# The opening of a hybrid decoder layer: norm sums from rows of tokens, one chunk unnormed, three products side by side

## The chip, the cores and the metric

The kernel runs on one core of a Trainium2 chip. The metric is the device time of one execution in microseconds (us), the median over runs. A core has five engines that take instructions in their own order and wait for each other through semaphores: TensorE (PE in the profile; its weight loads are PEld), VectorE (DVE), ScalarE (ACT), GpSimd (POOL) and SyncE (SP, which only issues DMAs here). GpSimd and ScalarE issue some DMAs too.

## The reference

One layer over 1,024 prompt tokens and 64 sample tokens (T = 1088), model width 1024, all in float32. The part that matters here is its beginning:

```
xn = rmsnorm(x, norm1_g)                  # x * rsqrt(mean(x*x) + eps) * g, per token
proj = xn @ w_in                          # q | k | v | glu_a | glu_b | gate_a | gate_b
u = glu_a * sigmoid(glu_b)                # then causal depthwise conv (31), layernorm, silu, w_pb
h = x + (sigmoid(gate_a) * A + sigmoid(gate_b) * B) @ w_out    # A: windowed attention, B: the conv branch
y = h + ConvFFN(rmsnorm(h))               # up, conv (3), silu gate, down; final rmsnorm
```

## The kernel before

Activations lie transposed: 128 channels on the partitions, tokens along the free axis, in KT = 8 slices k of the 1024 channels. Tokens are cut into three chunks of 384, 384 and 320 columns (`CHUNKS`). Every float32 operand is split into a high part (rounded to the matmul's type by a copy on ScalarE, `xh`, `whi`) and the rest (a subtraction on VectorE, `xl`, `wlo`); a product of one 128-column weight unit with one chunk is 24 matmuls, three per k: `wh*xh`, `wh*xl`, `wl*xh` (L183 to L185, `mm3`). A product over all three chunks is 72 matmuls. `SEQUENCE` gives the order of the input projection's 44 units: `b` and `a` are the two halves of the GLU, `g` gates, `q0` and `q1` queries, `k`, `v`. A `b`/`a` pair is followed by a depthwise convolution on VectorE (L452 and neighbours), which runs beside later products.

The opening is the first `FIRST` = 5 units, worked chunk by chunk rather than unit by unit, since x is not normed yet. `norm1_load` brings x by DMA on SyncE's queue, chunk 0 in pieces between the pieces of the first two weights; `norm1_raw` scales x by g only and splits it (L253, L254). The products run on that, and the factor 1/rms of the token (`rstd`) is multiplied in when a result leaves PSUM (`ev_b`, `ev_a`, `ev_q`, `gate_evac` with `self.scale`). `norm1_stats` makes the factor: squares on ScalarE (L263), their sum over k on VectorE (L265), the sum over partitions by a matmul with a constant matrix (L268), square root and a reciprocal over 128 x 384 elements (L283, L284). In chunk 0 the first two products run side by side, k by k, while x is still landing (`stream_side`). After each chunk's products the earlier chunk is normed in place for the 39 units that follow (`norm1`: L277 on VectorE, L278 on ScalarE, L280 in turn on VectorE and GpSimd). The last one, chunk 2, is normed after the fifth product.

The order on each engine is the tile framework's: it places instructions by priority, in the order of the program text, shifted by `later`; `issue_after` (new in the change) holds an instruction back behind a named one. An engine runs its own list strictly in order. PSUM has eight banks, four under the tag `mm` and four under `aux` (`FIRST_TAGS` deals them out); a product waits until its bank has been emptied. In the opening the raw weights lie in borrowed tiles (`u`, `c`), and the fifth split weight in the unused end of the query tiles `q`.

Of the kernel before, what the change touches and what calls it, by code (L numbers as in the profile page):

```python
# [12 lines left out]
P = 128  # L13
# [100 lines left out]
class Build:  # L114
# [29 lines left out]
    def w_split(self):  # L144
        if len(self.w_hl) < len(self.order):
            for go in self.w_parts(2 if len(self.w_hl) < FIRST else 1):
                go()
# [75 lines left out]
    def norm1_load(self, pp, c):  # L223
# [8 lines left out]
        self.w_raw += [self.t(self.wp, [P, DM], "wraw", bufs=2) for _ in range(2)]  # L232
        half = DM // 2
        w_part = lambda i, x: load(self.w_raw[i][:, x * half:(x + 1) * half], self.a["wall"][i][:, x * half:(x + 1) * half])
# [11 lines left out]
    def norm1_raw(self, c, xr, xh, xl):  # L246
        parts = list(zip(self.w_parts(W_PARTS), self.w_parts(W_PARTS))) if c == 0 else []
        for k in range(KT):
            if parts and k * W_PARTS % KT == 0:
# [7 lines left out]
    def norm1_stats(self, pp, c, xr):  # L257
        nc = self.nc
        n = CHUNKS[c][1]
        ps = self.bank("aux")  # L260
        for k in range(KT):
            sq = self.t(pp, [P, 384], "sq", bufs=SQ_BUFS)
            nc.scalar.activation(sq[:, :n], xr[:, k, :], AF.Square)  # L263
            if k:
                nc.vector.tensor_tensor(sq[:, :n], sq[:, :n], last[:, :n], ALU.add)  # L265
            last = sq
        with self.later(MEAN_LATER[c]):
            nc.tensor.matmul(ps[:, :n], self.mean, last[:, :n], start=True, stop=True)  # L268
        rstd = self.t(pp, [P, 384], f"rstd{c}")
        self.rstd(rstd[:, :n], ps[:, :n])  # L270
        return rstd

    def norm1(self, c, xr, rstd, xh, xl):
        nc = self.nc
        for k in range(KT):
            x = xr[:, k, :]
            nc.vector.scalar_tensor_tensor(x, x, self.c("g1", k), rstd[:, :CHUNKS[c][1]], ALU.mult, ALU.mult)  # L277
# [1175 lines left out]
```

## Time and profile before

| | |
|---|---|
| median of 3 runs | 1692.3 us (1691.95 to 1692.46) |
| the profiled execution | 1690.92 us, of which the span of instructions 1689.1 us |
| mean granted TensorE clock over the span | 0.997 |
| TensorE, VectorE, ScalarE, GpSimd busy | 1669.8, 1299.2, 842.3, 249.2 us |

The page gives busy time per engine, the chain of waits, the costliest groups of instructions by line, and the DMA issues. Other views of the same trace are a timeline of an engine, groups by line in a stretch, and a table of windows: for each stretch the busy time of each engine (with the count of instructions), the granted clock, the busy share of the 16 DMA engines, and GB/s. Matmuls overlap, so TensorE's "busy" is not a rate: what it does in a stretch is read from the number of matmuls.

### The profile page before, as it was taken

The page shows a single profiled execution, that of the slowest core. Times are in us where ns is not written, and L with a number is a line of the kernel's source. Part 1 is how long each engine was busy: PE and PEld are TensorE (multiplying, and loading weights), DVE is VectorE, ACT ScalarE, POOL GpSimd, SP SyncE. Part 2 cuts the span into 40 slices and gives each one's busy share as a digit, 9 for nine tenths or more (in the row PEclk, how much of TensorE's full clock was granted, in tenths as well). Part 3 has the DMA queues.
Part 4 walks back from the last instruction along what each step waited for, and adds up shares of the span by engine and source line. Part 5 has one row for each costly group of instructions (what it writes and reads, how often), then busy time and mean ns, then how long its engine had stood idle before and what let it go on. Part 6 is the DMA issues. An engine that isn't in the chain of part 4 may idle for free.

```text
span 1689.1 us, 29120 instructions
## 1 busy us (share of the span) xinstructions
PE 1669.8 (99%) x11372; PEld 1650.8 (98%) x11372; DVE 1299.2 (77%) x2265; ACT 842.3 (50%) x1711; POOL 249.2 (15%) x430
## 2 busy tenths in 40 slices
PE   9899999999999999999999999999999999999998
PEld 8899999999999999999999999999999999999997
DVE  8999989999679996865546887777777787754437
ACT  7424478753588745973233544444444455211102
POOL 1300212240011111110000261222222220000000
PEclk9999999999999999999999999999999999999999
DMA  6022212232211255644343333222222225843103
GB/s 209 30 63 71 74 62 98 82 123 58 82 45 51 78 215 170 178 152 151 110 144 106 93 106 103 78 77 78 78 77 78 90 66 164 257 119 103 52 1 106
DMA packets 103657, 172.16 MB, mean 102 GB/s; under 512 B 44336, under 2 KB 69312, under 8 KB 103504
## 3 DMA queue, kind: packets, MB, share of 16 engines
q1 hardware_dynamic: 89952, 125.15, 25.1%
q0 software_dynamic: 13424, 45.15, 7.3%
q8 instruction: 89, 1.46, 0.4%
q14 instruction: 48, 0.39, 0.1%
q10 hardware_dynamic: 144, 0.00, 0.0%
HBM read 124.74 MB, written 47.50 MB: 102 GB/s over the span
## 4 chain that ended last, share of the span: by engine, by line
PE 82%; DVE 11%; ACT 5%; issue 1%; DMA 1%; SPq 0%; DVEq 0%; ACTq 0%
PE mm L185 20%; PE mm L183 20%; PE mm L184 20%; PE aux L183 6%; PE aux L185 6%; PE aux L184 5%; DVE c L452 2%; ACT p L305 1%; DVE bt L452 1%; PE aux L338 1%; PE aux L351 1%; PE aux L350 1%; ACT p L309 1%; DVE xr L277 1%; PE aux L328 1%
## 5 line engine op out<-in xcount | busy, mean ns | idle before, releaser
L183 PE MATMUL mm<-xh,whi 128*128 128x384 f32 (+1 forms) x920 | 306.8, 334 | 5.0 <-DVE gt L649 2.3
L184 PE MATMUL mm<-xl,whi 128*128 128x384 f32 (+1 forms) x920 | 301.9, 328 | 0.7 <-DVE xl L254 0.5
L185 PE MATMUL mm<-xh,wlo 128*128 128x384 f32 (+1 forms) x920 | 300.9, 327 | 1.4 <-DVE wlo L165 1.4
L183 PEld LDWEIGHTS mm<-xh,whi 128*128 128x128 f32 x920 | 173.4, 189 | 7.4 <-ACT xh L278 2.6
L184 PEld LDWEIGHTS mm<-xl,whi 128*128 128x128 f32 x920 | 173.6, 189 | 3.0 <-DVE xl L254 1.9
L185 PEld LDWEIGHTS mm<-xh,wlo 128*128 128x128 f32 x920 | 173.1, 188 | 1.8 <-DVE wlo L165 1.7
L183 PE MATMUL mm<-mh,whi 128*128 128x272 f32 (+2 forms) x464 | 137.8, 297 | 0.0
L184 PE MATMUL mm<-ml,whi 128*128 128x272 f32 (+2 forms) x464 | 137.7, 297 | 0.0
L185 PE MATMUL mm<-mh,wlo 128*128 128x272 f32 (+2 forms) x456 | 135.3, 297 | 0.0
L164 ACT CAST whi<-wraw 128x1024 fp32r<-128x1024 f32 (+1 forms) x79 | 77.3, 984 | 114.2 <-PE mm L184 58.7
L1044 DVE SCALAR_TENSOR_TENSOR acc<-st,fc,acc 128x1104 f32<-128x1104 f32 x88 | 119.7, 1363 | 2.7 <-ACT acc L1042 2.0
L165 DVE TENSOR_TENSOR wlo<-wraw,whi 128x1024 fp32r<-128x1024 f32 (+1 forms) x79 | 89.6, 1139 | 19.0 <-ACT whi L164 17.7
L452 DVE SCALAR_TENSOR_TENSOR bt<-u,consts,bt 128x513 f32<-128x513 f32 x120 | 89.7, 747 | 0.6
L452 DVE SCALAR_TENSOR_TENSOR c<-sm,hsum,c 128x512 f32<-128x512 f32 x120 | 89.5, 745 | 0.4
L184 PEld LDWEIGHTS mm<-ml,whi 128*128 128x128 f32 x464 | 87.3, 188 | 0.0
L183 PEld LDWEIGHTS mm<-mh,whi 128*128 128x128 f32 x464 | 87.3, 188 | 0.0
L185 PEld LDWEIGHTS mm<-mh,wlo 128*128 128x128 f32 x456 | 85.7, 188 | 0.0
L452 DVE SCALAR_TENSOR_TENSOR c<-u,consts,c 128x512 f32<-128x512 f32 x112 | 83.4, 745 | 0.4
L185 PE MATMUL aux<-mh,wlo 128*128 128x272 f32 (+2 forms) x256 | 77.5, 303 | 0.0
L183 PE MATMUL aux<-mh,whi 128*128 128x272 f32 (+2 forms) x240 | 72.9, 304 | 0.0
L184 PE MATMUL aux<-ml,whi 128*128 128x272 f32 (+2 forms) x240 | 72.7, 303 | 0.0
L184 PE MATMUL mm<-tl,whi 128*128 128x272 f32 x240 | 69.6, 290 | 0.0
(386 smaller groups left out, 5199.3 us busy)
## 6 DMA issues: line engine op xcount, KB each, us to landing
wraw<-wall SPq DMA_DIRECT2D x130, 512.0 KB, 4.1
d_g<-acc POOLq DMA_DIRECT2D x22, 552.0 KB, 5.3
gr<-d_g SPq DMA_DIRECT2D x16, 512.0 KB, 4.9
ga<-d_ga SPq DMA_DIRECT2D x8, 544.0 KB, 4.0
gb<-d_gb SPq DMA_DIRECT2D x8, 544.0 KB, 3.7
mar<-d_ma SPq DMA_DIRECT2D x8, 544.0 KB, 5.1
xr<-xT SPq DMA_DIRECT2D x32, 136.0 KB, 2.6
d_h<-H POOLq DMA_DIRECT2D x4, 1088.0 KB, 5.9
```

Of the source, the lines that this page charges most:

```text
L164: self.nc.scalar.copy(h[:, z], r[:, z])
L165: self.nc.vector.tensor_tensor(l[:, z], r[:, z], h[:, z].bitcast(F32), ALU.subtract)
L183: mm(ps, wh, xh, start=first, stop=False, skip_group_check=more)
L184: mm(ps, wh, xl, start=False, stop=False, skip_group_check=more)
L185: mm(ps, wl, xh, start=False, stop=last, skip_group_check=more)
L277: nc.vector.scalar_tensor_tensor(x, x, self.c("g1", k), rstd[:, :CHUNKS[c][1]], ALU.mult, ALU.mult)
L305: nc.scalar.activation(pt[:, j, lo:width + 1], pt[:, j, lo:width + 1], AF.Exp, bias=nm[:, j:j + 1], scale=-1.0, accum_out=den[:, j:j + 1])
L309: nc.scalar.activation(pt[:, j, lo:width], pt[:, j, lo:width], AF.Identity, scale=den[:, j:j + 1])
L328: nc.tensor.matmul(ps[:, j, :], q[g][:, h, qs], kd[g][:, keys], start=True, stop=False)
L338: nc.tensor.transpose(ps[:, h * P:(h + 1) * P], pt[:, h, kb * P:(kb + 1) * P], self.ident)
L452: mac = lambda o, x, w: nc.vector.scalar_tensor_tensor(o, x, w, o, ALU.mult, ALU.add)
L1044: nc.vector.scalar_tensor_tensor(acc, st[:, k:k + AW], fw(f, k), acc, ALU.mult, ALU.add)
```

## The change

1. **Sums from rows.** A second layout of x, `xN` (tokens on the partitions), is passed in. `norm1_rows` loads a chunk as up to three tiles of 128 tokens x 1024 channels, ScalarE squares each with a running sum per partition (L291), one square root and one reciprocal over 128 x 3 numbers follow (L293, L294), and the factors go through memory: per tile a DMA of one number per partition into `d_r`, then one DMA that reads them back broadcast over 128 partitions (L297, L299), all on GpSimd's queue. The matmul with the constant matrix, the sums on VectorE and the wide reciprocals go.
2. **One chunk unnormed.** Only chunk 0 is split raw and scaled on leaving PSUM; chunks 1 and 2 are normed before their products, and their results leave by copies on ScalarE (`put`). Chunk 0 is normed last.
3. **Three gates among the first five.** The opening's units are b, a and three gates; the two queries move behind them. The queries' detour through `qt` goes.
4. **Three side by side** in chunk 0 where two were (`SIDE` = 3); the second and third weight's first halves are issued from ScalarE's DMA queue.
5. `queued` and `issue_after` hold the copies and the gates' stores of chunks 1 and 2 behind named instructions.

```
 SEQUENCE = (
-    "b a q0 g q0 b a q0 q0 k0 b a v v "
-    "g g b a g b a g g g b a "
-    "q1 q1 q1 g q1 k1 b a g b a g g g g g g g"
+    "b a g g g q0 q0 b a q0 q0 k0 b a v v "
+    "g b a g b a g g g b a "
+    "q1 q1 q1 q1 k1 b a g b a g g g g g g g"
 ).split()
...
-FIRST_TAGS = (("mm", "mm", "mm", "mm", "aux"), ("aux", "mm", "mm", "mm", "mm"), ("aux", "mm", "mm", "mm", "mm"))
-SQ_BUFS = 4
-QT_BUFS = 1
-MEAN_LATER = (100, 100, 100)
+SIDE = 3
+FIRST_TAGS = (("mm", "mm", "mm", "mm", "aux"), ("aux", "aux", "aux", "mm", "mm"), ("aux", "aux", "mm", "mm", "mm"))
+XT_BUFS = 3
...
+    @contextmanager
+    def queued(self, x):
+        with ExitStack() as es:
+            if self.behind is not None:
+                es.enter_context(self.tc.issue_after(self.behind[x]))
+            yield
+
+    def put(self, d, s):
+        with self.queued(0):
+            self.nc.scalar.copy(d, s)
...
         w_part(0, 0)
+        w_part(1, 0, self.nc.scalar.dma_start)
         x_part(0, 1)
-        w_part(1, 0)
+        w_part(2, 0, self.nc.scalar.dma_start)
         x_part(1, 2)
         x_part(2, 4)
-        w_part(0, 1)
-        w_part(1, 1)
+        for i in range(SIDE):
+            w_part(i, 1)
         x_part(4, 6)
         x_part(6, 8)
...
+    def norm1_rows(self, pp, c):
+        o, n = CHUNKS[c]
+        rows = []
+        for x in range(o, o + n, P):
+            m = min(P, o + n - x)
+            t = self.t(pp, [P, DM], "xt", bufs=XT_BUFS)
+            self.nc.sync.dma_start(t[:m], self.a["xN"][x:x + m])
+            rows.append((t, m))
+        return rows
+
+    def norm1_stats(self, pp, c, rows):
...
+        for i, (t, w) in enumerate(rows):
+            sq = nc.scalar.activation(t[:w], t[:w], AF.Square, accum_out=s[:w, i:i + 1])
+        r = s[:, :len(rows)]
+        nc.scalar.activation(r, r, AF.Sqrt, bias=self.c("eps", 0), scale=1.0 / DM)
+        nc.vector.reciprocal(r, r)
+        for i, (t, w) in enumerate(rows):
+            x = o + i * P
+            nc.gpsimd.dma_start(self.d_r[0:1, x:x + w].rearrange("a t -> t a"), s[:w, i:i + 1])
+        rstd = self.t(pp, [P, 384], "rstd", bufs=2)
+        load = nc.gpsimd.dma_start(rstd[:, :n], self.d_r[0:1, o:o + n].to_broadcast([P, n]))
+        return rstd, (sq.ins, load.ins)
...
-        xr = [self.norm1_load(p0, 0)]
+        xr[0] = self.norm1_load(p0, 0)
+        nc.scalar.activation(self.warm, self.warm, AF.Sqrt)
+        rows[1] = self.norm1_rows(p0, 1)
         self.w_load()
-        self.w_load()
+        xr[1] = self.norm1_load(p0, 1)
+        while len(self.w_raw) < FIRST:
+            self.w_load()
+        rows[0] = self.norm1_rows(p0, 0)
+        xr[2] = self.norm1_load(p0, 2)
...
+        self.norm1_raw(0, xr[0], xh, xl)
+        ws = [self.weight(w, 0) for w in self.order[:FIRST]]
+        evs = [ev_b, ev_a] + [gate_evac(*x) for x in self.order[2:FIRST]]
+        norm1 = lambda c: self.norm1(c, xr[c], rs[c], xh, xl)
+        stats(1)
+        norm1(1)
+        stats(0)
+        rows[2] = self.norm1_rows(p0, 2)
         for c in range(3):
-            self.norm1_raw(c, xr[c], xh, xl)
-            if not c:
-                ws = [self.weight(w, 0) for w in self.order[:FIRST]]
-            rs.append(self.norm1_stats(p0, c, xr[c]))
-            self.scale = rs[c]
-            evs, tags = (ev_b, ev_a, ev_q(0), gate_evac(*self.order[3]), ev_q(1)), FIRST_TAGS[c]
-            side = 0 if c else 2
+            side, tags = 0 if c else SIDE, FIRST_TAGS[c]
+            self.scale = None if c else rs[0]
             if side:
                 self.stream_side(xs, evs[:side], ws[:side], tags[:side], c)
-            for w, ev, tag in list(zip(ws, evs, tags))[side:]:
+            for x, (w, ev, tag) in list(enumerate(zip(ws, evs, tags)))[side:]:
+                if c:
+                    self.behind = normed if c == 1 and x > 2 else spread[2]
                 self.stream(None, xs, ev, chunks=(c,), w=w, tag=tag)
-            if c:
-                self.norm1(c - 1, xr[c - 1], rs[c - 1], xh, xl)
+            if c == 0:
+                stats(2)
+                normed = norm1(2)
+        self.behind = None
+        with tc.issue_after(normed[2]):
+            norm1(0)
         self.derive()
-        self.norm1(2, xr[2], rs[2], xh, xl)
```

How the change moves instructions, at the places that the prediction speaks of. A row is line, operation, out<-in and shape, with a count; `xh_20`, `xl_21` and `xr_35` are the changed kernel's chunk 1 (`xh_19`, `xl_20`, `xr_31` before), `xh_18` its chunk 0, `q_24`/`q_25` its fifth weight (high and low part; `q_23`/`q_24` before).

TensorE at the end of chunk 0's fifth product, before (the end of `aux_348`, then chunk 1's first product):

```order
L183 MATMUL aux_348<-xh_17_101,q_23_119 128x384
L184 MATMUL aux_348<-xl_18_102,q_23_119 128x384
L185 MATMUL aux_348<-xh_17_101,q_24_120 128x384
L183 MATMUL mm_449<-xh_19_103,whi_38_155 128x384
L184 MATMUL mm_449<-xl_20_104,whi_38_155 128x384
L185 MATMUL mm_449<-xh_19_103,wlo_39_156 128x384
```

and the beginning of the fifth product (`aux_387`) in the changed kernel:

```order
L184 MATMUL mm_359<-xh_18_101,wloy_216 128x384
L182 MATMUL aux_387<-xh_18_101,q_24_119 128x384
L183 MATMUL aux_387<-xl_19_102,q_24_119 128x384
L182 MATMUL aux_451<-xh_20_103,whi_43_167 128x384
L182 MATMUL aux_477<-xh_20_103,whi_45_169 128x384
L184 MATMUL aux_387<-xh_18_101,q_25_120 128x384
L182 MATMUL aux_387<-xh_18_101,q_24_119 128x384
```

Two matmuls of chunk 1 now stand ahead of the third matmul of chunk 0's fifth product, and 21 more of that product stand behind them.

VectorE where the fifth weight is split, before:

```order
L254 SCALAR_TENSOR_TENSOR xl_20_104<-xr_31_140,consts_74,xh_19_103 128x384 x7
L165 TENSOR_TENSOR q_24_120<-wraw_143,q_23_119 128x512 x2
L254 SCALAR_TENSOR_TENSOR xl_20_104<-xr_31_140,consts_74,xh_19_103 128x384
L265 TENSOR_TENSOR sq_398<-sq_398,sq_396 128x384
L265 TENSOR_TENSOR sq_401<-sq_401,sq_398 128x384
```

and in the changed kernel (`sum_53`, `rstd_236` are chunk 1's sums and factors):

```order
L294 RECIPROCAL sum_53_227<-sum_53_227 128x3
L164 TENSOR_TENSOR wloy_216<-c_145,whiy_215 128x512 x2
L306 SCALAR_TENSOR_TENSOR xr_35_147<-xr_35_147,consts_75,rstd_236 128x384 x3
L164 TENSOR_TENSOR q_25_120<-wraw_150,q_24_119 128x512 x2
L309 TENSOR_TENSOR xl_21_104<-xr_35_147,xh_20_103 128x384 x2
L306 SCALAR_TENSOR_TENSOR xr_35_147<-xr_35_147,consts_75,rstd_236 128x384 x4
```

The low part of the fifth weight now stands behind three instructions that read chunk 1's factors.

VectorE where chunk 0's results leave PSUM, before (`rstd_55` are chunk 0's factors):

```order
L284 RECIPROCAL rstd_55_234<-rstd_55_234 128x384
L265 TENSOR_TENSOR sq_404<-sq_404,sq_401 128x384
L759 TENSOR_TENSOR u_148<-mm_237,rstd_55_234 128x384
L762 TENSOR_TENSOR c_152<-mm_238,rstd_55_234 128x384
L767 TENSOR_TENSOR qt_314<-mm_289,rstd_55_234 128x384
L649 TENSOR_TENSOR gt_345<-mm_320,rstd_55_234 128x384
```

and in the changed kernel (`rstd_271` are chunk 0's factors, `sum_68` chunk 2's sums):

```order
L805 TENSOR_TENSOR u_162<-mm_279,rstd_271 128x384
L811 TENSOR_TENSOR c_166<-mm_280,rstd_271 128x384
L679 TENSOR_TENSOR gt_356<-mm_281,rstd_271 128x384
L679 TENSOR_TENSOR gt_384<-mm_359,rstd_271 128x384
L679 TENSOR_TENSOR gt_412<-aux_387,rstd_271 128x384
L294 RECIPROCAL sum_68_415<-sum_68_415 128x3
```

Chunk 2's reciprocal now stands behind the five instructions that read chunk 0's factors; the three `gt` tiles share two buffers, and each is stored by a DMA of GpSimd's queue.

GpSimd in the opening, before:

```order
L650 DMA d_ga_60<-gt_345 128x384
L280 ISA
L280 TENSOR_TENSOR xl_18_102<-xr_26_123,xh_17_101 128x384 x4
L650 DMA d_ga_60<-gt_531 128x384
L280 TENSOR_TENSOR xl_20_104<-xr_31_140,xh_19_103 128x384 x4
```

and in the changed kernel:

```order
L297 DMA d_r_60<-sum_53_227 128x1 x3
L299 DMA rstd_236<-d_r_60 128x384
L309 ISA
L309 TENSOR_TENSOR xl_21_104<-xr_35_147,xh_20_103 128x384 x4
L297 DMA d_r_60<-sum_55_262 128x1 x3
L299 DMA rstd_271<-d_r_60 128x384
L681 DMA d_ga_61<-gt_356 128x384
L681 DMA d_gb_62<-gt_384 128x384
L681 DMA d_ga_61<-gt_412 128x384
L297 DMA d_r_60<-sum_68_415 128x1 x2
L297 DMA d_r_60<-sum_68_415 64x1
L299 DMA rstd_425<-d_r_60 128x320
```

Twelve DMAs of factors are new on GpSimd's queue, in three groups of four (three stores, one load), and three stores of gates stand between the second and the third group.

More of the change, by code (lines that the diff above doesn't have):

```diff
@@ L145, in w_split @@
         if len(self.w_hl) < len(self.order):
[L146 removed]
+            for go in self.w_parts(1 + (len(self.w_hl) < FIRST)):
                 go()
@@ L255, in norm1_raw @@
                                                 ALU.mult, ALU.subtract)
-    def norm1_stats(self, pp, c, xr):
-        nc = self.nc
[L259 to L271, printed above, removed]
+    def norm1_rows(self, pp, c):
[8 more added lines that the diff above has]
+    def norm1_stats(self, pp, c, rows):
+        nc = self.nc
+        o, n = CHUNKS[c]
+        s = self.t(pp, [P, 4], f"sum{c}")
+        m = rows[-1][1]
+        if m < P:
+            nc.gpsimd.memset(s, 1.0)
+        for i, (t, w) in enumerate(rows):
[9 more added lines that the diff above has]
+        return rstd, (sq.ins, load.ins)
     def norm1(self, c, xr, rstd, xh, xl):
```

64 lines of the change are left out of this document (36 added, 28 removed).

## The prediction

> **What bounds the kernel now.** I read the page's busy times first, then a table of windows, then TensorE's own timeline.
>
> ```profile
> span 1689.1 us, 29120 instructions
> PE 1669.8 (99%) x11372; PEld 1650.8 (98%) x11372; DVE 1299.2 (77%) x2265; ACT 842.3 (50%) x1711; POOL 249.2 (15%) x430
> ```
>
> TensorE is the bound, and the change takes only the three matmuls of L268 from it. What can be won is time in which it waits. The windows (busy us and count per engine, granted clock, DMA share, GB/s) show where that is:
>
> ```profile
> 0.00:5.50 5.50, 4.44 (x25) 4.44 (x25) 1.11 (x5) 2.93 (x6) 1.04 (x7) 1.00 0.60 179
> 5.50:16.60 11.10, 9.89 (x50) 7.98 (x50) 10.16 (x22) 10.37 (x25) 0.16 (x2) 1.00 1.02 376
> 16.60:29.00 12.40, 12.40 (x71) 12.13 (x70) 12.30 (x25) 11.07 (x24) 0.00 (x0) 1.00 0.91 280
> 29.00:69.80 40.80, 40.74 (x250) 40.00 (x249) 40.46 (x64) 20.27 (x41) 12.73 (x10) 1.00 0.05 13
> 69.80:84.20 14.40, 8.49 (x33) 6.96 (x32) 14.21 (x27) 9.02 (x20) 6.45 (x9) 0.76 0.16 63
> 84.20:200.00 115.80, 115.80 (x770) 115.80 (x770) 114.36 (x185) 46.24 (x102) 11.04 (x23) 1.00 0.23 68
> 200.00:500.00 300.00, 296.38 (x1876) 289.37 (x1875) 263.24 (x545) 190.96 (x464) 59.48 (x106) 1.00 0.26 79
> ```
>
> 16.6 to 29 is TensorE at its rate: 71 matmuls of 384 columns in 12.4 us, 0.175 us each. By that rate the 50 of 5.5 to 16.6 are 8.7 us of work (2.4 lost, waiting for x and weights to land and be split), and the 33 of 69.8 to 84.2 are 5.8 us (8.6 lost). In 29 to 69.8 about 0.5 is lost. VectorE is busy 14.21 of 14.4 us in the bad stretch and 114.36 of 115.8 after it: there TensorE waits for VectorE, which is late because it sums squares, takes reciprocals and norms three chunks.
>
> ```profile
> 5.47 0.42 PE L183 MATMUL mm<-xh,whi 128*128 128x384 f32 x1
> 61.00 0.81 PE L268 MATMUL aux<-sq,mean 128*128 128x320 f32 x2
> 61.40 0.55 PE L183 MATMUL aux<-xh,whi 128*128 128x320 f32 x1
> 73.83 0.60 PE L183 MATMUL mm<-xh,whi 128*128 128x320 f32 x1 [2.26 <-DVE gt L649]
> 76.70 0.69 PE L183 MATMUL mm<-xh,whi 128*128 128x384 f32 x1 [1.62 <-DVE qt L767]
> 83.96 0.44 PE L185 MATMUL mm<-xh,wlo 128*128 128x384 f32 x1 [1.40 <-DVE wlo L165]
> ```
>
> The first product starts at 5.5 us; a sum by matmul takes 0.4 us, three 1.2. **Lost before, up to 84.2 us: 5.5 + 2.4 + 0.5 + 1.2 + 8.6 = 18.2 us.** Behind 84.2 TensorE is busy throughout until 200, and idle 3.6 us between 200 and 500.
>
> **The change, part by part.** First what VectorE sheds, from the groups by line in 0 to 85 us (count | busy us, mean ns):
>
> ```profile
> L277 DVE SCALAR_TENSOR_TENSOR xr<-xr,consts,rstd 128x384 f32<-128x384 f32 (+1 forms) x24 | 17.7, 771 | 0.0
> L254 DVE SCALAR_TENSOR_TENSOR xl<-xr,consts,xh 128x384 fp32r<-128x384 f32 (+1 forms) x24 | 13.8, 616 | 0.8 <-ACT xh L253 0.7
> L265 DVE TENSOR_TENSOR sq<-sq,sq 128x384 f32<-128x384 f32 (+1 forms) x21 | 11.1, 527 | 0.3
> L284 DVE RECIPROCAL rstd<-rstd 128x384 f32<-128x384 f32 (+1 forms) x3 | 7.2, 2409 | 0.0
> L767 DVE TENSOR_TENSOR qt<-mm,rstd 128x384 f32<-128x384 f32 (+1 forms) x5 | 2.6, 520 | 0.0
> ```
>
> All of L265 and L284, 16 of 24 of L254 (9.2 us) and L767 go: some 30 us of VectorE's work. The norming (L277) stays. This removes the cause of the 8.6 us, but the factors now come by a trip through memory, and each of the three trips has TensorE waiting behind it.
>
> Loading. The rate of the loads now, and the clock in the bad stretch, from windows of 5 us:
>
> ```profile
> 0.00:5.00 5.00, 3.94 (x20) 3.94 (x21) 0.68 (x4) 2.43 (x5) 1.04 (x7) 1.00 0.58 178
> 5.00:10.00 5.00, 4.69 (x25) 3.41 (x24) 4.10 (x9) 4.27 (x12) 0.00 (x0) 1.00 0.96 333
> 10.00:15.00 5.00, 4.11 (x22) 3.46 (x21) 4.90 (x12) 5.00 (x12) 0.00 (x0) 1.00 1.05 401
> 15.00:20.00 5.00, 5.00 (x30) 5.00 (x30) 5.00 (x14) 5.00 (x12) 0.16 (x2) 1.00 1.06 379
> 20.00:25.00 5.00, 5.00 (x29) 4.73 (x28) 5.00 (x10) 3.71 (x8) 0.00 (x0) 1.00 1.00 301
> 70.00:75.00 5.00, 2.10 (x7) 1.18 (x6) 4.91 (x12) 3.97 (x8) 1.36 (x2) 0.79 0.34 137
> 75.00:80.00 5.00, 3.38 (x12) 3.30 (x12) 4.94 (x10) 3.82 (x11) 1.90 (x2) 0.52 0.08 33
> 7.97 1.12 ACT L253 ACTIVATE xh<-xr,consts 128x384 fp32r<-128x384 f32 x2 [0.73 <-DMA xr<-xT]
> ```
>
> In all 0.9 MB have moved by 5 us, 2.6 by 10, 4.6 by 15, 6.5 by 20, 8.0 by 25. Counting sizes in order of issue, x's third piece ended at 1.31 MB, moved by 6.3 us, and ScalarE took it at 7.97; earlier pieces lag by about 1. I add 1.2 us to land.
>
> *Start.* ScalarE now splits a piece of three weights before the first slice of x: 1.18 MB (three half weights, two slices), so 5.9 + 1.2 + 0.4 (a cast) + 0.6 (xh, half of the 1.12) = **8.1 us**, from 7.5 to 8.8. From there three products side by side use each slice for 9 x 0.175 = 1.6 us instead of 1.05, so x (all landed by 13) is ahead: lost in chunk 0 **0**, up to 1. They end at 8.1 + 72 x 0.175 = 20.7; the fourth weight (5.2 MB, landed by 18, split by 20) is in time, and the fourth product ends at 24.9.
>
> *The first trip.* The rows of chunk 1 are at 4.7 MB, landed at 16.6.
>
> ```profile
> 74.42 1.06 ACT L616 ACTIVATE u<-u 128x1024 f32<-128x1024 f32 x1
> L305 ACT ACTIVATION_READ_ACCUMULATOR p<-p,nm x30: 185/187/193, 193.5 to 259.7; 128x1 f32 x30
> L650 POOL DMA_DIRECT2D d_ga<-gt x24: 540/542/705, 31.2 to 638.4; - x24
> o_cbp<-u POOLq DMA_DIRECT2D x1, 15.0 KB, 1.9
> d_c<-u POOLq DMA_DIRECT2D x1, 32.0 KB, 3.3
> d_gb<-gt POOLq DMA_DIRECT2D x1, 192.0 KB, 2.1
> d_gb<-gt POOLq DMA_DIRECT2D x1, 160.0 KB, 4.4
> wraw<-wall SPq DMA_DIRECT2D x1, 512.0 KB, 4.0
> 36.77 2.96 DVE L277 SCALAR_TENSOR_TENSOR xr<-xr,consts,rstd 128x384 f32<-128x384 f32 x4
> 22.80 1.28 DVE L165 TENSOR_TENSOR q<-wraw,q 128x512 fp32r<-128x512 f32 x2
> ```
>
> A square over 128 x 1024 is not in the trace; the nearest row is 1.06 us, with the read of the sum 1.25. The last one ends at 17.9, root and reciprocal (tiny) at 18.4. The third store is issued at 19.5 (0.54 each). A DMA of GpSimd lands 1.9 (small) and 2.1 us (192 KB) after its issue on a quiet machine; issued beside a weight load (the 160 KB one, with the 4.0 us load) it took 4.4, a small one 3.3. So the factors arrive at 19.5 + 1.9 + 0.1 + 2.1 = 23.6 at best, at 19.5 + 3.3 + 0.1 + 4.4 = 27.3 loaded. The loads run without pause here (share 1.00 at 20 to 25, and the change adds 4.4 MB), so I take **27.2**. Behind them VectorE norms three slices (0.53 each) and splits half a weight (0.64): TensorE's third matmul of the fifth product waits from 25.2 to 29.6, less two matmuls 4.0 us. At the best price it is 0.6. In the bad stretch the clock fell to 0.79 and 0.52 after such waits, 3.5 us in sum over two of them; I count half, 1.7. **5.7**, from 0.6 to 7.5.
>
> [...]
>
> *Chunk 1.* VectorE needs 8 x 0.53 + 4 x 0.47 + 1.2, and 0.8 for each of about two slices that GpSimd subtracts at the same time (the four L277 above took 2.96, not 2.2): 9 us from 27.2, so the last slice is there at 36.5. The fifth product ends at 29.6 + 22 x 0.175 + 1.7 = 35.2, and the next needs its last slice 3.6 later. **0.5**, up to 2. Chunk 1 ends at 56.3.
>
> *The second and third trip.* ScalarE's root for chunk 0 stands behind the eight casts of chunk 1: 36.8. The bytes are through at about 41, so the stores cost something and the load nothing extra: factors at 37.0 + 1.1 + 2.6 + 0.1 + 2.1 = 42.9. Five results leave by VectorE, but the third gate needs a `gt` buffer back, a store of 0.54 + 2.1 later; chunk 2's reciprocal is at 47.3, its factors at 52.5, the first slice at 53.6. TensorE comes at 56.3: no wait, but VectorE needs 8.5 us for eight slices and the first product eats them in 3.5: **1.5**, up to 5.5 if both trips are loaded.
>
> *The sixth weight's low part* stood late before (1.40) and again has the GLU product and the convolution's first instruction ahead of it: **1.0**, up to 2.5.
>
> Lost after: 8.1 + 5.7 + 0.5 + 1.5 + 1.0 = 16.8, so the opening gives 18.2 - 16.8 = **1.4**. The 30 us that VectorE is ahead can only win what TensorE still waits later, the 3.6 idle us of 200 to 500; the queries, and so the attention, come two products later and have eleven instead of twelve products before the second group. I take **2.1**, from 3.6 won to 2 lost.
>
> The span becomes 1689.1 - 3.5 = 1685.6, the execution (1.8 more, as 1690.92 has) 1687.4. The median of the runs is 1.4 above the profiled one: **1688.8 us**.
>
> **The rivals.**
> *The trips are cheap.* If small DMAs pass the loads, the first factors come at 23.6: 0.6 instead of 5.7 at the fifth product, all else as above. 3.5 + 5.1 less about 1 (TensorE then reaches chunk 2 earlier, near the factors): 1684.7. For it: GpSimd's DMAs use a queue of their own. Against: 4.4 and 3.3 beside one load.
> *The trips are a serial chain* (slower). Each factor starts the next: casts of chunk 1, root of chunk 0, results of chunk 0, reciprocal of chunk 2. If every store and load costs the loaded price, chunk 2's factors come at 37 + 8.9, + 4.4, + 8.9 = 59.2, first slice 60.3, 4 us after TensorE, which is idle long enough for another 1.7 and then eats slices faster than VectorE makes them (2 more): 1688.8 + 7.7 = 1696.5. It decides from 55.2 on for the factors. For it: the third trip's stores queue behind three stores of gates on GpSimd. Against: the loads are over by 41.
> *Given back later.* The opening wins 1.4, but the attention's eleven products leave a wait as long as the gain: 1692.
> *Twice the time at half clock.* The bad stretch shows 3.5 us lost to the clock; if the one wait of 4.4 us costs as much, it is 1.7 more, 1690.5. For it: the wait is longer than any of the three there. Against: they were three. [...]
>
> **How the numbers follow.** Forecast 0.42 (own range 1686 to 1691.5), cheap 0.25, chain 0.18, given back 0.10, clock 0.05. 0.2% is 3.4 us, about what a measurement of this kernel can tell from no change: faster means below 1688.9, slower above 1695.7. Faster: half of the forecast and all of cheap, 0.46. Slower: most of the chain and a little of given back, 0.16. Same: 0.38. The range takes in cheap and most of the chain: 1683 to 1696.
>
> **What would show it.** First product at 8.1; no gaps from there to 24.9; one wait of 4 us at the fifth product's L184, ended by VectorE's `q`, with a clock below 1 behind it; the three loads of `rstd` landing at 27, 43 and 52; chunk 2's first matmuls without a wait of over 1 us; no stretch like 69.8 to 84.2. The prediction is wrong if the stores or loads of factors take under 2.2 or over 4.5 us, if x is late for three products, or if TensorE's idle time between 200 and 500 grows.

## The result, and the profile after

| | before | after |
|---|---|---|
| median of 4 runs each | 1692.12 us (1691.40 to 1692.46) | 1716.62 us (1715.56 to 1717.29) |
| ratio, 95% interval | | 1.0145 (1.0127 to 1.0162) |
| span of the profiled execution | 1689.1 us | 1714.9 us |

The change costs 24.5 us where 3.5 were forecast to be won. The page of the changed kernel shows that the engines do what was foreseen (VectorE's busy time falls by 25.3 us), and that the span is longer all the same:

```profile
span 1714.9 us, 29070 instructions
PE 1673.3 (98%) x11366; PEld 1656.8 (97%) x11366; DVE 1273.9 (74%) x2219; ACT 834.1 (49%) x1696; POOL 260.8 (15%) x443
```

The windows of the changed kernel, with borders laid at TensorE's waits (busy us and count per engine, granted clock, DMA share, GB/s):

```profile
24.30:37.40 13.10, 1.30 (x4) 0.50 (x2) 1.19 (x3) 1.66 (x4) 0.54 (x1) 0.61 0.85 239
37.40:55.60 18.20, 18.07 (x93) 17.37 (x94) 9.89 (x18) 11.20 (x23) 8.09 (x7) 0.91 0.38 111
55.60:61.30 5.70, 0.39 (x4) 0.07 (x2) 0.63 (x2) 0.00 (x0) 0.55 (x1) 1.00 0.28 37
61.30:71.20 9.90, 9.90 (x48) 9.83 (x48) 1.96 (x5) 0.48 (x1) 3.21 (x6) 0.83 0.16 61
71.20:80.00 8.80, 0.25 (x2) 0.00 (x0) 0.98 (x3) 0.40 (x1) 1.14 (x2) 0.71 0.23 41
80.00:90.00 10.00, 9.53 (x47) 9.20 (x48) 9.96 (x17) 6.25 (x16) 6.05 (x7) 0.74 0.10 39
```

Three holes, in which VectorE does next to nothing either (1.2, 0.6 and 1.0 us). By count and rate (0.175 us for a matmul of 384 columns, and in proportion 0.146 for the 320 of the last row) the six windows lose 12.4, 1.9, 5.0, 1.5, 8.5 and 3.1 us; with the 7.5 us ahead of the first product that is 39.9 us, against 18.2 before and 16.8 forecast. So 21.7 of the span's 25.8 us lie here. TensorE's timeline names what each hole waited for (start, duration, in brackets the idle time and what ended it). The first hole has two parts, the fifth weight (`q`, landed at 28.8 us) and then chunk 1's normed slices:

```profile
7.54 0.62 PE L182 MATMUL mm<-xh,whi 128*128 128x384 f32 x2 [0.99 <-ACT xh L269]
29.51 0.69 PE L182 MATMUL aux<-xh,q 128*128 128x384 f32 x1 [4.92 <-ACT q L163]
37.43 1.01 PE L182 MATMUL aux<-xh,whi 128*128 128x384 f32 x2 [6.91 <-ACT xh L307]
61.28 0.69 PE L182 MATMUL mm<-xh,whiy 128*128 128x384 f32 x1 [5.31 <-DVE u L805]
80.11 0.90 PE L182 MATMUL aux<-xh,whi 128*128 128x320 f32 x2 [8.66 <-ACT xh L307]
485.40 1.35 PE L368 MATMUL aux<-consts,p 128*128 128x128 f32 x4 [3.65 <-ACT p L339]
```

The other releasers (`xh` of a normed chunk, `u` out of PSUM) each waited for factors. The table of waits from 15 to 90 us (total, times, longest) gives the chain one step further back:

```profile
DVE xr L306 <- DMA rstd<-d_r: 30.3, 2, 16.6
POOL rstd L299 <- DMA d_r<-sum: 25.7, 3, 10.3
...
DVE u L805 <- DMA rstd<-d_r: 13.1, 1, 13.1
```

25.7 us go by between the issue of the last store of a trip and its landing, in three trips. The DMA issues of the changed kernel (size of one, median us from issue to landing):

```profile
rstd<-d_r POOLq DMA_DIRECT2D x2, 192.0 KB, 4.9
rstd<-d_r POOLq DMA_DIRECT2D x1, 160.0 KB, 3.9
d_r<-sum POOLq DMA_DIRECT2D x8, 0.5 KB, 7.9
d_r<-sum POOLq DMA_DIRECT2D x1, 0.2 KB, 7.4
```

A store of half a kilobyte takes 7.9 us, and the view of its line gives 7.1 to 10.4 for the nine. The second trip's stores are under way while the DMA engines move next to nothing (0 GB/s from 50 to 55 us), the third's beside 40 GB/s (66 to 80 us), so other traffic hardly explains them.

### The profile page after: what moved, and what is told of

It is laid out like the page before. It is cut to its first block, busy times and chain, and to the rows that moved or that the text cites. A ratio compares the mean times of both kernels' runs of the same rounds, so it can differ in the third digit from the quotient of the medians.

```text
span 1714.9 us, 29070 instructions
## 1 busy us (share of the span) xinstructions
PE 1673.3 (98%) x11366; PEld 1656.8 (97%) x11366; DVE 1273.9 (74%) x2219; ACT 834.1 (49%) x1696; POOL 260.8 (15%) x443
## 4 chain that ended last, share of the span: by engine, by line
PE 86%; DVE 6%; DMA 4%; ACT 2%; issue 1%; POOL 0%; DVEq 0%; SPq 0%; ACTq 0%; POOLq 0%
PE mm L182 21%; PE mm L184 21%; PE mm L183 21%; PE aux L183 5%; PE aux L184 5%; PE aux L182 5%; PE aux L368 2%; DMA d_r<-sum 1%; DVE c L482 1%; DMA rstd<-d_r 1%; PE aux L380 1%; DMA wraw<-wall 1%; PE aux L358 1%; PE aux L381 1%; PE aux L359 1%
## 5 line engine op out<-in xcount | busy, mean ns | idle before, releaser
L182 PE MATMUL mm<-xh,whi 128*128 128x384 f32 (+1 forms) x904 | 301.7, 334 | 1.0 <-ACT xh L269 1.0
L184 PE MATMUL mm<-xh,wlo 128*128 128x384 f32 (+1 forms) x904 | 296.1, 328 | 0.0
L183 PE MATMUL mm<-xl,whi 128*128 128x384 f32 (+1 forms) x904 | 296.0, 327 | 0.0
L163 ACT CAST whi<-wraw 128x1024 fp32r<-128x1024 f32 (+1 forms) x79 | 77.5, 985 | 115.7 <-PE mm L183 59.2
L335 ACT ACTIVATE p<-p,nm 128x257 f32<-128x257 f32 (+1 forms) x128 | 62.3, 490 | 15.3 <-DVE nm L330 14.9
```

What stands on the lines that cost most here:

```text
L163: self.nc.scalar.copy(h[:, z], r[:, z])
L182: mm(ps, wh, xh, start=first, stop=False, skip_group_check=more)
L183: mm(ps, wh, xl, start=False, stop=False, skip_group_check=more)
L184: mm(ps, wl, xh, start=False, stop=last, skip_group_check=more)
L335: nc.scalar.activation(pt[:, j, lo:width + 1], pt[:, j, lo:width + 1], AF.Exp, bias=nm[:, j:j + 1], scale=-1.0, accum_out=den[:, j:j + 1])
```

## The experiments

**The form of the store.** First the stores alone were changed, in three ways.

```
-            nc.gpsimd.dma_start(self.d_r[0:1, x:x + w].rearrange("a t -> t a"), s[:w, i:i + 1])
+        nc.vector.transpose(sT, s)
+        for b in range(4):
...
+            nc.gpsimd.dma_start(d[:, 32 * b:32 * b + 32], sT[32 * b:32 * b + m, :])
```

> The changed kernel, with one edit: VectorE transposes the factors in blocks of 32 x 32 first, so that a chunk's factors go to memory as 12 runs of 32 numbers (four DMAs of three runs) and not as 384 single numbers (three DMAs of 128). Theory A (single numbers are what is slow: 7.1 to 10.4 us from issue to landing in the changed kernel): the stores land within 3 us of their issue, the three rstd loads end at about 28, 52 and 64 us instead of 36.2, 60.6 and 79.0, the waits of 5 us at 55.6 and of 8.8 us at 71.1 all but go, and the time is 1696 to 1704 us. If single numbers also slow the loads beside them, the fifth weight lands near 24 us instead of 28.8. Theory B (GpSimd's queue, or the count of its DMAs, is what is slow): four DMAs take 7 us or more as three did, 1715 to 1720 us. Theory C (the 4.4 MB of added loads are what delays the first trip): the first trip stays at 36 and the fifth weight at 28.8; second and third trip as now.

1700.96 us in one run (the kernel before beside it: 1692.64). The stores in this kernel's DMA issues (three runs each, then two):

```profile
d_r<-sumT POOLq DMA_DIRECT2D x10, 0.4 KB, 3.5
...
d_r<-sumT POOLq DMA_DIRECT2D x2, 0.2 KB, 1.5
```

The edit alone takes back 15.7 of the 24.5 us. Theory A holds where the machine is quiet: the second and third factors come at 51.8 and 63.8 us, as it said. The first trip's stores, beside the loads, still take up to 6.3 us, and its factors come at 32.0 us, not 28. The hole at 55.6 us is gone, that of the third trip is shorter but there; the two waits that are left:

```profile
33.27 0.69 PE L184 MATMUL aux<-xh,q 128*128 128x384 f32 x1 [6.70 <-DVE q L164]
64.87 0.55 PE L182 MATMUL aux<-xh,whi 128*128 128x320 f32 x2 [3.91 <-ACT xh L309]
```

The loads gain as well. The windows from 20 to 30 us of the changed kernel, and then of this one, end in GB/s:

```profile
20.00:25.00 5.00, 4.59 (x27) 4.27 (x25) 0.00 (x0) 0.00 (x0) 0.05 (x1) 1.00 1.34 308
25.00:30.00 5.00, 0.49 (x2) 0.50 (x2) 0.00 (x0) 1.14 (x2) 0.00 (x0) 0.71 0.73 173
```

```profile
20.00:25.00 5.00, 5.00 (x30) 5.00 (x30) 0.00 (x0) 0.17 (x1) 0.90 (x2) 1.00 1.04 400
25.00:30.00 5.00, 1.57 (x10) 1.25 (x8) 0.00 (x0) 0.97 (x2) 0.58 (x1) 0.87 1.08 362
```

With single numbers on their way the loads move 2.4 MB in these 10 us, without them 3.8; the fifth weight lands at 24.8 instead of 28.8 us. Theory C, that the added loads hold up the trip, could at most explain the first one.

```
+        nc.gpsimd.dma_start(self.d_r[0:1, o:o + m * P].rearrange("a (i t) -> t (a i)", t=P), s[:, :m])
```

> The changed kernel, with one edit: a chunk's factors are stored by one DMA of 384 single numbers instead of three of 128. Theory A: the price goes by the single numbers, so that one DMA takes the 7 to 8 us that three took together on a quiet machine; about 1 us is saved in issuing per trip; 1712 to 1717 us. Theory B (the price goes by the DMA): one takes 2.5 to 4 us, 1700 to 1706 us.

1720.23 us in one run, above both ranges: one DMA of 384 numbers takes 8.9 to 12.7 us, as long as three of 128 together or longer. Theory B's price per DMA falls.

```
-            nc.gpsimd.dma_start(self.d_r[0:1, x:x + w].rearrange("a t -> t a"), s[:w, i:i + 1])
+            nc.scalar.dma_start(self.d_r[0:1, x:x + w].rearrange("a t -> t a"), s[:w, i:i + 1])
```

> The changed kernel, with one edit: the factors' stores are issued on ScalarE's DMA queue instead of GpSimd's (the load stays on GpSimd's). Theory A: they take 6 to 10 us there too, 1713 to 1719 us. Theory B: 2 to 3 us, as other small transfers, 1698 to 1704 us.

1726.65 us in one run, outside both ranges: 7.1 to 17.1 us per store. GpSimd's queue is not the cause.

**The price by itself.** A chain of single transfers in the kernel before, each followed by a load that waits for it (`r` is a tile of 128 partitions, `d` one in memory):

```
+        dma(d[0:1, :].rearrange("a t -> t a"), r[:, 0:1])           # 128 single numbers
+        for i in range(3):                                         # 384
+            dma(d[0:1, i * P:i * P + P].rearrange("a t -> t a"), r[:, i:i + 1])
+        dma(d, r[:, 0:16])                                          # runs of 16, of 128
...
+        for b in range(4):                                         # 12 runs of 32
+            dma(d[:, 32 * b:32 * b + 32], r[32 * b:32 * b + 3, 0:32])
```

> The kernel before, with a chain of stores and loads added on GpSimd's queue behind the second GLU product (some 120 us in, where the loads of the opening are over); each store is followed by a load that waits for it. The stores: 128 single numbers by one DMA; 384 by three DMAs; 128 runs of 16 numbers; 128 runs of 128 numbers; 12 runs of 32 numbers by four DMAs; 128 single numbers again. Theory A: the 384 single numbers take 7 to 8 us; 128 of them either as long (a fixed price of the form) or about a third, 2.5 to 3 us (a price per number); the runs of 16 and of 128 numbers and the 12 runs take 2 to 3 us. Theory B: every store on this queue takes about as long, and the form decides nothing. The time of this kernel is no evidence: GpSimd's own work waits behind the chain.

Its DMA issues (KB, us from issue to landing; 64B and 512B are runs of 16 and 128 numbers; the first store once more, at the end of the chain, took 8.7):

```profile
e_512B<-gt POOLq DMA_DIRECT2D x1, 64.0 KB, 1.8
...
e_128B<-gt POOLq DMA_DIRECT2D x4, 0.4 KB, 2.5
...
e_three<-gt POOLq DMA_DIRECT2D x3, 0.5 KB, 9.2
e_one<-gt POOLq DMA_DIRECT2D x1, 0.5 KB, 8.9
e_64B<-gt POOLq DMA_DIRECT2D x1, 8.0 KB, 1.7
```

128 times the bytes (64 KB) cost a fifth of the time. And 128 single numbers cost as much as 384: not a price per number either. Two reasons were left, the size of a write and its neighbours:

```
+        for name, n in (("e_by_64B", 16), ("e_by_512B", P)):
+            d = dram([P, n], name)
+            dma(d[:, 0:1], r[:, 0:1])
...
+        for name, n in (("e_run_2", 2), ("e_run_4", 4), ("e_run_8", 8)):
+            d = dram([P, n], name)
+            dma(d, r[:, 0:n])
```

> The kernel before, with a second chain of stores and loads on GpSimd's queue behind the second GLU product: 128 single numbers side by side in memory (8.8 us in the first list); 128 single numbers 64 bytes apart; 512 bytes apart; then 128 runs of 2, 4 and 8 numbers, side by side (runs of 16 took 1.7 us). Theory S (a write of 4 bytes is slow in itself): all single numbers take 8 to 9 us wherever they go, and the price falls with the length of the run. Theory N (neighbours that share a line of memory hinder each other): single numbers 64 or 512 bytes apart take about 2 us, and runs of 2 to 8 are slow like the first. The time of this kernel is no evidence.

Singles side by side 9.2 us, at 64 bytes 2.6, at 512 bytes 1.8. Runs of 2, 4 and 8 numbers, side by side, took 3.1, 1.8 and 1.7. A write of four bytes is not slow in itself: theory S falls. Theory N's guess that runs of 2 to 8 are slow like single numbers did not hold either. A third list varied the distance of single numbers alone (8, 16, 32, 64, 512 bytes):

> The kernel before, with a third chain of stores and loads on GpSimd's queue behind the second GLU product: 128 single numbers side by side; then 128 single numbers 8, 16, 32, 64 and 512 bytes apart; then side by side again. Theory N (neighbours that share a stretch of memory hinder each other; 9.2 us side by side, 2.6 us at 64 bytes, 1.8 us at 512): the price falls step by step with the distance, 5 us or less at 8 bytes, about 2 us from 64 bytes on, and is 8 to 9 us again in the last one. Rival (what counts is that the whole goes to one row of 512 bytes in memory, one piece after the other): 8 us still at 8 and 16 bytes, or a fall that the distance does not order. The time of this kernel is no evidence.

```profile
e_one<-gt POOLq DMA_DIRECT2D x1, 0.5 KB, 8.8
e_by_8B<-gt POOLq DMA_DIRECT2D x1, 0.5 KB, 5.9
...
e_by_16B<-gt POOLq DMA_DIRECT2D x1, 0.5 KB, 1.7
...
e_by_512B<-gt POOLq DMA_DIRECT2D x1, 0.5 KB, 1.7
...
e_again<-gt POOLq DMA_DIRECT2D x1, 0.5 KB, 7.6
```

The same 128 pieces of four bytes cost 8.8 us side by side and 1.7 to 1.8 at each distance from 16 bytes on. That fits theory N, with a nearer limit than was expected: what costs is that pieces of different partitions lie closer than 16 bytes. At 8 bytes the length of the piece counts too, 5.9 us for single numbers and 3.1 for runs of two. What does it inside the memory path no run shows.

**Without the trip.** Factors spread by TensorE: the identity matrix times the column on VectorE, then a matmul with the constant matrix (entries 1/1024). Chunk 0's results are taken out after two products of chunk 1.

```
+            nc.vector.tensor_scalar(rstd[:w, i * P:i * P + w], self.ident[:w, :w], s[:w, i:i + 1], None, ALU.mult)
...
+                nc.tensor.matmul(ps[:, x:x + w], self.mean[:w], rstd[:w, x:x + w], start=True, stop=True)
+        nc.scalar.activation(rstd[:, :n], ps[:, :n], AF.Identity, scale=float(DM))
```

> The changed kernel with no trip through memory: VectorE multiplies the identity matrix by the column of factors (three blocks of 128), three matmuls with the constant matrix spread them over all partitions, ScalarE copies the result out of PSUM (times 1024). Chunk 0's results are taken out behind the first two products of chunk 1, when its factors are there; TensorE takes nine 128-column matmuls more. Theory A (the trips are the whole loss in the opening): the factors of chunk 1 are there at about 21 us instead of 36.2, the waits at 24 to 37 us (12.3), at 55.6 (5.5) and 71.1 (8.8) and the half clocks behind them (some 5 us) go, about 1.5 us remain for the fifth weight (landed 24.8 when no single numbers were stored); 1686 to 1692 us. Rival (norming chunks 1 and 2 ahead of their products is itself too slow: VectorE makes a slice in 1.1 us and a product eats one in 0.53): TensorE waits for xl or xh at the start of chunks 1 and 2, 3 to 5 us each with the clock, 1695 to 1700 us. The wait of 3.8 and 2.3 us at 481 us stays in either case (about 10 to 30 us earlier).

1690.06 us (1688.14 to 1692.70), ratio to before 0.9985 (0.9976 to 0.9995). The three holes are gone; TensorE's waits up to 90 us are now:

```profile
7.44 0.62 PE L182 MATMUL mm<-xh,whi 128*128 128x384 f32 x2 [1.33 <-ACT xh L271]
27.11 0.44 PE L182 MATMUL aux<-xh,q 128*128 128x384 f32 x1 [1.93 <-ACT q L163]
29.73 0.69 PE L184 MATMUL aux<-xh,q 128*128 128x384 f32 x1 [1.13 <-DVE q L164]
```

So the trips were worth 26.6 us (the new place of chunk 0's results included), more than the whole loss, and norming chunks 1 and 2 ahead of their products is quick enough: the rival falls. What is left is the fifth weight (`q`), 3.1 us. It landed at 23.7 us here, but ScalarE split it at 26.45 only.

```
-            for k in range(0, KT, 4):
-                x_part(k, k + 4)
+            x_part(0, 4)
+            if c == 1:
+                self.w_load()
+            x_part(4, 8)
```

> As e6_matmul_later_turn, with the fifth weight loaded ahead of the second half of chunk 1's x instead of behind it. Theory: the fifth weight lands at about 22 instead of 24.8 us, and what TensorE waits for it at the fifth product of chunk 0 (about 1.5 us) goes; the second half of x comes at 25 and is not waited for, since VectorE reaches it about then; 1 to 2 us below e6_matmul_later_turn. Rival: x's second half is late for the norming of chunk 1, and the time stays or grows by 1 us.

1684.50 us (1683.19 to 1685.18), ratio 0.9952 (0.9937 to 0.9966): faster than both kernels, by 8.0 and 32.1 us. It has the lowest median of all kernels here. The weight lands at 21.1 us. Against e6_matmul_later_turn the gain is 5.1 us, not 1 to 2; the windows of that kernel and then of this one show where it comes from:

```profile
24.50:40.00 15.50, 12.47 (x61) 11.82 (x60) 9.98 (x22) 7.94 (x17) 4.54 (x4) 0.89 0.97 302
```

```profile
24.50:40.00 15.50, 15.38 (x89) 15.06 (x88) 10.53 (x23) 8.87 (x18) 4.98 (x4) 1.00 1.00 304
```

28 matmuls more in the same 15.5 us, 4.9 us of work: about 3.1 of it two waits as in e5_by_matmul's rows, the rest the clock, 0.89 over the stretch with them and 1.00 without. The theory was that the weight lands too late. ScalarE's timelines, of e6_matmul_later_turn and then of this kernel, say otherwise:

```profile
27.87 0.51 ACT L318 CAST xh<-xr 128x384 fp32r<-128x384 f32 x1 [0.48 <-DVE xr L317]
28.29 1.14 ACT L163 CAST q<-wraw 128x512 fp32r<-128x512 f32 x2
```

```profile
25.51 1.14 ACT L163 CAST q<-wraw 128x512 fp32r<-128x512 f32 x2
```

In e6_matmul_later_turn the weight landed at 24.8 us, 3.5 us before its split, which stood behind five casts of the norming. With the earlier load the split stands behind two of them. So the waits went with the place in ScalarE's list, which the earlier load moved; the landing alone is not shown to matter. The control with FIRST_UNIT as it was (e14_control, below) lies 3.7 us under e5_by_matmul.

**The order on TensorE.**

```
+                with tc.issue_after(prev) if c == 1 else ExitStack():
+                    mm = self.stream(None, xs, ev, chunks=(c,), w=w, tag=tag)
```

> The changed kernel, with one edit: every product of chunk 1 is held behind the fifth product of chunk 0 on TensorE (issue order alone). In the changed kernel the first matmuls of two products of chunk 1 stand ahead of the third matmul of that fifth product, so that 22 matmuls (3.9 us) which need no factor wait for the first trip as well. Theory: they now run while the trip is under way, from 29.5 to about 34 us; the wait for the factors (36.2 us) shrinks to about 3.5 us; 1712 to 1714 us. Rival (what TensorE wins there it loses behind it, since chunk 1's slices are not there faster, or to the clock): 1715 to 1718 us.

1718.17 us (1717.48 to 1720.25), ratio to before 1.0146 as the changed kernel's 1.0145: the rival's side. The 22 matmuls did not run during the trip. TensorE's and VectorE's timelines of this kernel say why:

```profile
39.70 0.69 PE L184 MATMUL aux<-xh,q 128*128 128x384 f32 x1 [13.62 <-DVE q L164]
```

```profile
37.37 1.67 DVE L307 SCALAR_TENSOR_TENSOR xr<-xr,consts,rstd 128x384 f32<-128x384 f32 x3 [17.86 <-DMA rstd<-d_r]
38.96 1.28 DVE L164 TENSOR_TENSOR q<-wraw,q 128x512 fp32r<-128x512 f32 x2
```

The fifth weight's low part needs no factor, but stands behind three norming instructions on VectorE's list, which do. VectorE idles 17.9 us with that work in its queue, some 13 of them with the high part already made (ScalarE's cast began at 24.8). In this kernel the weight itself landed at 24.8 us, although the single numbers were stored: which load they delay varies; the last piece of x landed at 36.8 us as in the changed kernel (36.7), against 32.7 with runs of 32.

**The wait at 485 us.** The gain that was forecast downstream did come: the kernel before has a wait of 2.19 us in the first attention group, which the changed kernel lacks.

```profile
206.85 0.51 PE L351 MATMUL aux<-ptl,v 128*128 128x512 f32 x1 [2.19 <-DVE ptl L213]
```

A new wait of 3.65 us at the first transposes of the second attention group took it back, with a clock of 0.89 from 470 to 500 us. Most theories of that wait fell. First, more time for the softmax:

```
-FIRST_UNIT = (10, 0)
+FIRST_UNIT = (10, 8)
```

> As e5_by_matmul, and the first unit of the second attention group transposes its probabilities 8 slices of a product later (FIRST_UNIT (10, 8) instead of (10, 0)). Theory: the wait of 3.8 us at 481 comes from softmax standing behind the last convolution on VectorE, one product nearer since a gate was moved from there to the opening; with 8 slices (4.2 us) more it goes: 3 to 5 us below e5_by_matmul. Rival (the wait belongs to the whole group, whose units all come late): it moves to the next unit, and the time stays within 1 us of e5_by_matmul.

1689.62 us (1687.31 to 1690.91), 0.4 below e5_by_matmul, the rival's side: the wait goes, and one of 1.84 us for `pth` comes instead. Then the order of the units:

```
-    "g b a g b a g g g b a "
-    "q1 q1 q1 q1 k1 b a g b a g g g g g g g"
+    "g b a g b a g g b a "
+    "q1 q1 q1 g q1 k1 b a g b a g g g g g g g"
```

> As e7_matmul_weight_earlier, but with FIRST_UNIT back at (10, 0) and a gate put back among the four queries ahead of the second attention group (taken from the four products ahead of the last GLU pair of the first group), so that six products instead of five stand between the last convolution's GLU product and the second group's first softmax, as in the kernel before. Theory (the waits around 470 us are the price of the gate that was moved to the opening): no wait of over 1.2 us from 440 to 490 us, against one of 3.8 in e5_by_matmul and one of 2.0 in e7_matmul_weight_earlier; 1681 to 1683.5 us. Rival (the first group, now with ten products, ends late instead): a wait at its end of 2 us or more, 1684 to 1687 us.

1687.76 us (1685.79 to 1688.49), in neither range; the wait is 3.85 us, so the gate's place among the queries is not the cause.

```
+    "g g b a g b a g g g b a "
+    "q1 q1 q1 q1 k1 b a g b a g g g g g g"
```

> As e10_gate_back (FIRST_UNIT (10, 0)), but the gate put ahead of the second attention group is taken from the last nine products, so that seventeen products instead of sixteen lie between the values and that group (eighteen in the kernel before). Theory (VectorE's convolutions of the first half have too few products to hide behind: the last one ends at 440.8 us in the kernel before, 18 us ahead of that group's first softmax, but at 450 to 478 us in the others, right before it): the last convolution ends 10 us or more ahead of the softmax, the wait of 4.0 us goes to under 1.2 us, and the time is 2 to 5 us below e10_gate_back, unless the second group, with one product fewer, leaves as much at its own end. Rival (the wait is the first unit's own: scores, root of the table and softmax take longer than its 14 slices, whatever VectorE does): a wait of 3 us or more stays.

1689.26 us (1687.73 to 1692.20), a wait of 3.3 us. But the convolution still ended behind the group's first scores, so the theory was not tested. What it does show: twelve products lie ahead of the group's queries again, as in the kernel before, and the wait stays. The next two went together:

```
+    "g b a g b a g b a g g "
+    "q1 q1 q1 q1 k1 b a g b a g g g g g g g"
```

> e7_matmul_weight_earlier with FIRST_UNIT back at (10, 0) and nothing else. What it adds to e5_by_matmul is the earlier fifth weight alone (theory: 4 to 5 us below e5_by_matmul, 1685 to 1686.5 us; rival, that the two edits only win together: 1688 us or more). What it lacks of e7_matmul_weight_earlier is the later turn alone. The wait at the transposes near 455 us is 3.5 to 4 us again.

> As e14_control, but the last GLU pair ahead of the second attention group stands two products earlier (b a g g where g g b a stood), so that its convolution can be done sooner; the number of products and the gates' share of them stay. Theory (VectorE still works on that convolution when the group's first scores come out of TensorE: first softmax instruction 0.7 us after the scores began in the kernel before, 5.2 us in e12_product_more, where the convolution ended 2.5 us after the scores began): the convolution ends ahead of the scores, the first softmax instruction follows within 1 us, the wait at the transposes is under 1.2 us, and the time is 2 to 5 us below e14_control. Rival (whatever VectorE does, TensorE comes too soon): a wait of 3 us or more stays, within 1 us of e14_control.

Control 1686.40 us (1684.86 to 1688.91), the pair moved 1685.88 (1684.98 to 1686.60); waits of 3.65 and 2.62 us. The convolution ran past the scores once more. At last its work was taken away:

```
-        for j in range(1, 16):
+        for j in range(1, 2 if i == 4 else 16):
```

> As e14_control, but 14 of the 15 steps of the convolution of the last GLU pair ahead of the second attention group are left out (42 instructions of VectorE, some 28 us). Theory (VectorE's backlog): VectorE is done with that convolution before the group's first scores; its first softmax instruction follows them within 1 us, as in the kernel before, the wait of 3.65 us at the transposes goes to under 1 us, and the time is 3 to 5 us below e14_control, 1681 to 1683.5 us. Rival (TensorE comes too soon whatever VectorE does): the wait stays at 2.5 us or more, 1685 to 1688 us.

1686.52 us (1685.70 to 1686.99), and the wait is 3.85 us, though the convolution now ends before the first score (444.3 and 444.45 us): VectorE's backlog is not the cause. VectorE's timeline of this kernel shows it idle just there, taking `k`'s low parts (`kl`) out one by one behind ScalarE, with the softmax's first instruction (the last row) in line behind the fourth:

```profile
446.51 0.55 DVE L735 TENSOR_TENSOR kl<-mm,kd 64x384 fp32r<-64x384 f32 x1 [1.58 <-ACT kd L733]
448.61 0.56 DVE L735 TENSOR_TENSOR kl<-mm,kd 64x384 fp32r<-64x384 f32 x1 [1.55 <-ACT kd L733]
449.21 0.35 DVE L343 CUSTOM_DVE_ANT_0 p<-aux,masks,nsink 128x128 f32<-128x128 f32 x1
```

That points to when the scores come. The first `kl` and the first score, in the timelines of the kernel before and then of the changed one:

```profile
447.79 0.55 DVE L688 TENSOR_TENSOR kl<-mm,kd 64x384 fp32r<-64x384 f32 x1 [1.22 <-ACT kd L686]
454.76 0.28 PE L328 MATMUL aux<-kd,q 128*128 128x256 f32 x1
```

```profile
470.33 0.55 DVE L723 TENSOR_TENSOR kl<-mm,kd 64x384 fp32r<-64x384 f32 x1
472.41 0.28 PE L358 MATMUL aux<-kd,q 128*128 128x256 f32 x1
```

Before, TensorE's list has the scores 7.0 us behind the first `kl`, now 2.1, and 2.1 to 2.7 in every experiment of this section; the transposes follow 42 product matmuls later before and after. So TensorE seems to ask some 5 us too soon, while `k` still leaves PSUM; the place of the softmax behind the fourth `kl` on VectorE would explain the wait as well. No kernel here put the scores back or moved the softmax ahead, so the cause is read from the traces and stays open.

## Why the prediction was wrong, point by point

- *What bounds the kernel, start and chunk 0.* As said: first product at 7.5 (8.1 forecast, 7.5 the low end), no gap of note until the fourth product's end at 24.3 (24.9).
- *The first trip: the step that failed.* "A DMA of GpSimd lands 1.9 (small) and 2.1 us (192 KB) after its issue on a quiet machine", 3.3 and 4.4 loaded. The store took 7.1 to 10.4 us, the load 3.9 to 5.8. Factors at 27.2, 42.9 and 52.5 became 36.2, 60.6 and 79.0. So the mechanism (TensorE waits behind each trip) was right and the price of a trip was not. The rows used as nearest (15 KB of `o_cbp`, 32 KB of `d_c`) were the smallest at hand and have as many pieces, 128, but pieces of 120 and 256 bytes; the form that mattered, adjacent single numbers from different partitions, stood in no row, and the upper bound should not have been taken from rows of another form. In the price lists the same half kilobyte took 1.7 to 2.6 us in single numbers 16 to 512 bytes apart, 7.6 to 9.2 in adjacent ones.
- *The wait at the fifth product.* Right place and mechanism (e9_order shows the low part behind the norming), 5.7 forecast, 14.3 measured with the clock. (The sum itself slips by 0.2: three slices and half a weight behind 27.2 end at 29.4, not 29.6.) That the fifth weight's own split would come late was not costed; e5_by_matmul puts that at 3.1 us, which the longer trip hid.
- *The second trip.* Forecast: "the stores cost something and the load nothing extra", and no wait of TensorE. Measured: a wait of 5.3 us. What is late was not named: chunk 1's fourth product needs a bank that chunk 0's result still holds, and `u` leaves it by the factors.
- *The third trip, and the rival of the chain.* 1.5 us forecast, 8.7 measured, and 3.1 lost behind it. The chain rival was the right mechanism (each trip starts the next, factors after 55.2 decide), priced at 59.2 for factors that came at 79.0, and so at 1696.5.
- *The clock.* 1.7 us forecast for the one wait; 1.9, 1.5 and 3.1 lost behind the three holes, most of it by the clock (0.91, 0.83, 0.74). Behind the waits of 4.9 and 6.9 us it was 0.50, from 30 to 40 us. But in e6_matmul_later_turn it also fell, to 0.59 from 32 to 36 us (0.89 over 24.5 to 40), behind waits of 1.9 and 1.1 us, and e5_by_matmul has 0.89 over the same stretch with waits of 1.93 and 1.13. So these runs show a lower clock behind short waits as behind long ones, and no length of wait that decides it; that one wait costs half of the 3.5 us was the author's estimate.
- *The sixth weight.* 1.0 forecast; no such wait in the changed kernel.
- *Downstream.* 2.1 us of gain forecast; the wait of 2.19 us at 207 did go, and one of 3.65 us at 485 came. From the opening to the last matmul that reads `xh` (648.3 us before, 671.9 after) 1.8 us more are lost, and 2.2 behind it, which no run explains. The rival "given back later" named a wait of this size, by luck: its cause, eleven products ahead of the second group, is not borne out, for with twelve again (e12_product_more) and with VectorE relieved (e15_short_convolution) the wait stayed.

## What to carry to other kernels

Price a transfer by the form of its pieces, not by its bytes: a column of single numbers that becomes a row in memory took 7.1 to 10.4 us in the changed kernel, where 32-number runs after a transpose took 1.5 to 3.5 (up to 6.3 beside the loads) and the way by a diagonal matrix and a matmul needs no transfer at all. When a step waits for such a trip, read what is queued behind the wait on each engine; in e9_order work that needed nothing from it (a weight's low part) stood still for some 13 us. A short wait of TensorE can cost its length and then the clock behind it: removing 3.1 us of waits gave 3.7 to 5.1, the second with a clock of 1.00 instead of 0.89 from 24.5 to 40 us.

## What the hardware showed that was not expected

128 four-byte writes from 128 partitions took 8.8 us side by side, 5.9 us 8 bytes apart, 1.7 to 1.8 us from 16 bytes on (one measurement at most distances; side by side five, 7.6 to 9.2; a second one at 64 bytes gave 2.6). 384 of them took about as long as 128 (9.2). While they ran beside the loads, the DMA engines' busy share was counted as 1.34 and they moved 308 GB/s, against 1.04 and 400 with runs of 32. And a load that spreads one row of half a kilobyte over 128 partitions (64 KB landed) took 3.6 to 4.5 us in the price lists, where 64 KB from 128 rows took 2.1.
